# Attention queries split for a two-pass product: the second copy of their high parts, by ScalarE or by a DMA between partitions

## The chip, the cores and the metric

The kernel runs on one core of a Trainium2 chip. The time is that of the device in microseconds for one execution of the whole program; the median of several runs counts. A core has a matrix engine (TensorE, called PE, with its weight loads listed as PEld), a vector engine (VectorE, DVE), an activation engine (ScalarE, ACT), a general engine (GpSimd, POOL) and a queue engine (SyncE, SP) that here issues the DMAs. Each engine works through its own list of instructions in order, and waits on semaphores for the others.

## What is computed

The reference is one step of a streaming encoder layer, in float32: a prompt of 1024 positions, and eight sample sequences of 16 new positions with 1024 cached keys each. Three residual parts follow one another. The edit lies in the first, in the differential attention of the prompt: four heads, each with two maps of 64 columns for queries and keys, whose softmaxes are subtracted.

```python
def diff_attend(q, k, v, bias, mask, lam):
    s = jnp.einsum('bqhmd,bkhmd->bhmqk', q, k).astype(jnp.float32) * (HEAD_DIM ** -0.5)
    s = jnp.where(mask, s + bias[None, :, None], NEG_INF)
    p = jax.nn.softmax(s, axis=-1)
    w = p[:, :, 0] - lam * p[:, :, 1]
    return jnp.einsum('bhqk,bkhe->bqhe', w.astype(v.dtype), v)
...
    h = rmsnorm(x, g_mix)
    z = h @ w_in
    zq, zk, zv, zu = jnp.split(z, [QK_COLS, 2 * QK_COLS, 2 * QK_COLS + ATTN_WIDTH], axis=-1)
    q = rmsnorm(zq.reshape(B, T, N_HEADS, 2, HEAD_DIM), g_q)
    k = rmsnorm(zk.reshape(B, T, N_HEADS, 2, HEAD_DIM), g_k)
...
    o = (rmsnorm(o, g_sub) * (1.0 - lam_init)).reshape(B, T, ATTN_WIDTH)
...
    x = x + jnp.concatenate([o, cv], axis=-1) @ w_out
    x = x + cross_attend(rmsnorm(x, g_cross), mk, mv, w_mq, g_mq, w_mo)
    hf = rmsnorm(x, g_ffn)
    x = x + jnp.square(jax.nn.relu(hf @ w_ff1)) @ w_ff2
```

A mask lets a query see the chunks of 64 up to its own. The samples go through the same attention with their cached keys and values in front.

## The kernel before

**Stages.** Up to about 284 us the input projection and the convolution run. Then comes the attention stage, to about 600 us. Four streams are woven together in it, written as generators: the prompt's attention (`prompt_stream`), the samples' attention (`sample_stream`, eight samples, each reading 2 MB of keys and 2 MB of values), the norm of the convolution (`conv_norm`), and the keys and values of the memory (`memory_stream`). The output projection follows; its convolution half (`pj` out of `wo` and `MT`) needs nothing of the attention and may run before it ends. After it come the cross attention and the MLP.

**Order.** The program is written by a framework that schedules: it takes the instructions as they are written, with priorities, runs them through a timeline of its own, and fixes the order on each engine by when an instruction would be ready there. An edit that changes one instruction's engine or duration can so change the order of others, on all engines, for as long as the streams are woven. At run time the order on an engine is fixed, and an instruction that waits holds up all behind it.

**The prompt's queries and keys.** A float32 product is made of rounded high parts and the low parts that are left. For a head h and a chunk c of 512 positions, `prep_queries` transposes four tiles of queries into one PSUM bank `ps` (`qst`, L619); its partitions 0 to 63 belong to map 0, 64 to 127 to map 1. For map m, with its half `a` of the partitions and the other half `b`, the tile `qs[:, m, :]` holds the scaled high parts twice, in both halves (L639 and L640), and `ql[a, m, :]` the low parts (L641), the rest of `ql` being zero. The keys in `kS[:, m, :]` hold high parts in `a` and low parts in `b` (L628, L629). One matmul of `qs` with `kS` (L674) gives high times high plus high times low at once, and one of `ql` with `kS` (L675) low times high. Both halves of `qs` must so be there before the first of them.

**Tiles of the prompt.** Each head has eight tiles i of 128 queries. `attend` makes two score tiles `sc` (map 0 and 1), adds the bias and finds the maximum on DVE (L679), and takes the exponential on ScalarE (L681); `values` transposes the weights (`pT`, L699), copies them (`wT`, L701) and multiplies by the values (`po`, L704), and stores the result to `mix` (L716). A preparation is made eight times, for each head and each half of its tiles, ahead of tiles 0 and 4.

**Memory.** `wT` lies in a pool (`wk2`) that is opened in the attention stage and takes over the memory of the convolution's accumulators `acc`. The last accumulator is worked on by DVE into the attention stage (L307), and stored to `dacc` (L331) once it is done.

**Samples.** For sample b, `sample_keys` transposes the cached keys (`kT`, L768, one PSUM bank), ScalarE copies them (`ku`, L770), and PE multiplies (`ss`, L777); `sample_weights` and `sample_values` make the weights (`wt`) and the values (`spo`, out of the loads `vu`). The results are stored to `ds`.

The functions that the edit touches, and those that call them:

Of the kernel before, what the change touches and what calls it, by code (L numbers as in the profile page):

```python
# [12 lines left out]
AF = mybir.ActivationFunctionType  # L13
# [46 lines left out]
def f32(ap):  # L60
    return ap.bitcast(F32)
# [3 lines left out]
def kernel(  # L65
# [8 lines left out]
    act, dve, pool, pe, sp = nc.scalar, nc.vector, nc.gpsimd, nc.tensor, nc.sync  # L74
# [357 lines left out]
    gqk = cst.tile([P, 1], F32, name="gqk")  # L432
# [182 lines left out]
    def flipped(r, name):  # L615

        ps = bk("tr", name)
        for j in range(4):
            pe.transpose(ps[:, j * P:(j + 1) * P], r[:, j, :], ident)  # L619
        return ps  # L620
# [11 lines left out]
    def prep_queries(h, c):  # L632

        ps = flipped(halves[0, h, c], f"qst{h}_{c}")
        qs = wk.tile([P, 2, 512], R32, name=f"qs{h}_{c}", tag="qs", bufs=AB["qs"])
        ql = qlow[c]
        for m in range(2):
            a, b = HALF[m], HALF[1 - m]
            act.activation(qs[a, m, :], ps[a], AF.Copy, scale=gqk[a])  # L639
            act.activation(qs[b, m, :], ps[a], AF.Copy, scale=gqk[a])  # L640
            dve.scalar_tensor_tensor(out=ql[a, m, :], in0=ps[a], scalar=gqk[a], in1=f32(qs[a, m, :]),  # L641
                                     op0=ALU.mult, op1=ALU.subtract)
        qss[h, c] = (qs, ql)
        yield
# [6 lines left out]
    def prep(h, c):  # L651

        for wi in (1, 0):
            if (wi, h, c) not in halves:
                load_half(wi, h, c)
        prep_values(h, c)
        yield from prep_keys(h, c)
        yield from prep_queries(h, c)
# [787 lines left out]
    def w1_ops(pr):  # L1446

        raw = []
        for kh in range(2):
            r = next(w1raw).rearrange("p (k c) -> p k c", k=4)  # L1450
            sp.dma_start(r, w_ff1[0, kh * 512:(kh + 1) * 512, pr * 256:(pr + 1) * 256].rearrange("(k p) c -> p k c", p=P))
            raw.append(r)
        a11, a21, a12, a22 = (raw[kh][:, :, f * P:(f + 1) * P] for kh in range(2) for f in range(2))
        s3 = kc(rpool.tile([P, 512], F32, name=f"s3_{pr}", tag="r"))
        ops = {}

        def op(nm, src):
            ops[nm] = wpool.tile([P, 2, 512], R32, name=f"{nm}_{pr}", tag="w")
            split_op(ops[nm].rearrange("p h (k c) -> p h k c", k=4), src)

        if NS <= pr < 16 - NL:
            op("a11", a11)
            op("a12", a12)
        dve.tensor_sub(s3, a11, a21)
        dve.tensor_add(a21, a21, a22)
        dve.tensor_sub(a11, a21, a11)
        op("s2", a11)
        op("s3", s3)
        op("s1", a21)
        op("a22", a22)  # L1470
        dve.tensor_sub(a12, a12, a11)
        op("s4", a12)
        return ops
# [43 lines left out]
    for pr in range(16):  # L1517
# [6 lines left out]
        a = nxt or w1_ops(pr)  # L1524
# [42 lines left out]
    def bank2(name):  # L1567
        return pps.tile([P, 512], F32, name=name, tag="ps")
# [40 lines left out]
    for nm, an, bn, change in STEPS:  # L1609
        ps = [bank2(f"{nm}_{i}") for i in range(4)]  # L1610
# [94 lines left out]
```

## Time and profile before

| | us |
|---|---|
| median of 3 runs | 1568.92 |
| lowest and highest run | 1566.68, 1574.23 |
| profiled execution, its time | 1571.44 |
| profiled execution, span from the first to the last instruction | 1569.7 |

Busy in the span: PE 1496.6 us, DVE 1084.4 us, ScalarE 731.9 us, GpSimd 243.6 us. An engine that is busy only now and then can still be what another waits for. A row of a timeline gives the start and the duration in us, the engine, the line, the operation and the names as out<-in; in square brackets stands how long the engine was idle before it, and what ended the idle time. Rows with SPq are DMAs being issued, and the duration is that of the issue alone.

### The profile page before, as it was taken

How to read it: one execution, taken by the hardware profiler on the slowest of the kernel's cores; microseconds unless marked ns; L12 is line 12 of the kernel's file. 1: busy time of each engine (PE TensorE's matmuls, PEld its weight loads, DVE VectorE, ACT ScalarE, POOL GpSimd, SP SyncE). 2: the span in 40 equal slices, each digit the busy share in tenths (PEclk: the TensorE clock that was granted, in tenths of full speed). 3: DMA queues.
4: the chain of work that ended last, by engine and by line, in shares of the span. 5: the costliest groups of instructions: out<-in, count | busy, mean ns of one | idle time of the engine just before them, and what ended most of it. 6: DMA issues, size and time to landing. Idle time of an engine off the chain costs nothing. (4 is left out here: it accounts for less than half of the span.)

```text
span 1569.7 us, 25622 instructions
## 1 busy us (share of the span) xinstructions
PE 1496.6 (95%) x9326; PEld 1297.6 (83%) x9326; DVE 1084.4 (69%) x2008; ACT 731.9 (47%) x1530; POOL 243.6 (16%) x374
## 2 busy tenths in 40 slices
PE   7999999789898899999999899999999999999999
PEld 7989898557686787887779899999999788878887
DVE  5899899967666564535758786666566556996565
ACT  6312021478677742635656354444353444544342
POOL 3152530041544431131011000000000000000000
PEclk9999999899999999999999999999999999999999
DMA  6423242578774733112432554543574567743443
GB/s 206 139 82 108 87 141 110 170 253 258 231 230 150 254 108 106 46 47 73 155 110 90 166 188 154 160 149 126 167 225 143 173 206 225 237 128 111 122 137 94
DMA packets 187121, 237.88 MB, mean 152 GB/s; under 512 B 23851, under 2 KB 101717, under 8 KB 186996
## 3 DMA queue, kind: packets, MB, share of 16 engines
q1 hardware_dynamic: 186996, 236.25, 47.4%
q8 instruction: 73, 1.20, 0.3%
q14 instruction: 52, 0.43, 0.1%
HBM read 172.59 MB, written 63.60 MB: 150 GB/s over the span
## 5 line engine op out<-in xcount | busy, mean ns | idle before, releaser
L124 PE MATMUL p<-Bp,Ap 128*128 128x512 f32 x448 | 174.9, 390 | 1.1 <-DVE Bp L1573 1.1
L125 PE MATMUL p<-Bp,Ap 128*128 128x512 f32 x448 | 174.2, 389 | 0.0
L123 PE MATMUL p<-Bp,Ap 128*128 128x512 f32 x448 | 157.8, 390 | 1.9 <-ACT Bp L1572 1.9
L307 DVE SCALAR_TENSOR_TENSOR acc<-cp,wc,acc 128x1024 f32<-128x1024 f32 (+2 forms) x150 | 159.1, 1068 | 0.7
L1572 ACT CAST Ap<-w_xb 128x512 fp32r<-128x512 f32 x112 | 69.5, 621 | 160.4 <-PE p L125 133.6
L1573 DVE TENSOR_TENSOR Ap<-w_xb,Ap 128x512 fp32r<-128x512 f32 x112 | 77.8, 694 | 90.2 <-ACT Ap L1572 90.1
L123 PE MATMUL p<-b_t,s 128*128 128x288 f32 x384 | 114.9, 299 | 4.0 <-DVE o L1419 4.0
L125 PE MATMUL p<-b_t,s 128*128 128x288 f32 x384 | 114.6, 299 | 0.5 <-DVE s L1326 0.5
L124 PE MATMUL p<-b_t,s 128*128 128x288 f32 x384 | 114.7, 299 | 0.0
L124 PEld LDWEIGHTS p<-Bp,Ap 128*128 128x128 f32 x448 | 84.1, 188 | 20.5 <-DVE Bp L1573 3.0
L123 PEld LDWEIGHTS p<-Bp,Ap 128*128 128x128 f32 x448 | 83.9, 188 | 19.9 <-ACT Bp L1572 2.7
L125 PEld LDWEIGHTS p<-Bp,Ap 128*128 128x128 f32 x448 | 84.1, 188 | 17.5
L123 PE MATMUL z<-wqkv,h 128*128 128x512 f32 x216 | 86.4, 400 | 0.0
L124 PE MATMUL z<-wqkv,h 128*128 128x512 f32 x216 | 85.5, 396 | 0.0
L125 PE MATMUL z<-wqkv,h 128*128 128x512 f32 x216 | 85.4, 396 | 0.0
L123 PEld LDWEIGHTS p<-b_t,s 128*128 128x128 f32 x384 | 73.2, 191 | 4.7 <-ACT s L1325 4.7
L1409 ACT ACTIVATE o<-o 128x576 f32<-128x576 f32 x64 | 43.9, 686 | 69.0 <-DVE o L1419 28.1
L123 PE MATMUL p<-b_b,a 128*128 128x288 f32 x256 | 75.8, 296 | 0.0
L124 PE MATMUL p<-b_b,a 128*128 128x288 f32 x256 | 75.7, 296 | 0.0
L125 PE MATMUL p<-b_b,a 128*128 128x288 f32 x256 | 75.7, 296 | 0.0
L125 PEld LDWEIGHTS p<-b_t,s 128*128 128x128 f32 x384 | 73.2, 191 | 0.8 <-DVE s L1326 0.8
L124 PEld LDWEIGHTS p<-b_t,s 128*128 128x128 f32 x384 | 73.3, 191 | 0.0
(511 smaller groups left out, 4239.8 us busy)
## 6 DMA issues: line engine op xcount, KB each, us to landing
kr<-in_cache_k_dram SPq DMA_DIRECT2D x32, 512.0 KB
vu<-in_cache_v_dram SPq DMA_DIRECT2D x32, 512.0 KB
w1t<-in_w_ff_dram SPq DMA_DIRECT2D x32, 512.0 KB
w_xb<-ds SPq DMA_DIRECT2D x64, 256.0 KB
da<-o SPq DMA_DIRECT2D x48, 256.0 KB
w_xb<-da SPq DMA_DIRECT2D x48, 256.0 KB
ds<-o SPq DMA_DIRECT2D x32, 256.0 KB
dxr<-XP SPq DMA_DIRECT2D x18, 256.0 KB
```

Source lines behind the costliest of these rows:

```text
L123: pe.matmul(out, lh, rh, start=first, stop=False)
L124: pe.matmul(out, lh, rl, start=False, stop=False)
L125: pe.matmul(out, ll, rh, start=False, stop=last)
L307: dve.scalar_tensor_tensor(out=out, in0=cp[:, lo + j:hi + j], scalar=wj, in1=out, op0=ALU.mult, op1=ALU.add)
L1409: act.activation(c, c, AF.Relu)
L1572: act.copy(u[:, 0], src)
L1573: dve.tensor_sub(u[:, 1], src, f32(u[:, 0]))
```

## The change

The second ScalarE operation on the same PSUM bank goes. In its place SyncE issues a DMA that copies the half `a` of the tile `qs` into its half `b`, from SBUF to SBUF across 64 partitions, 2 KB for each.

```diff
         for m in range(2):
             a, b = HALF[m], HALF[1 - m]
             act.activation(qs[a, m, :], ps[a], AF.Copy, scale=gqk[a])
-            act.activation(qs[b, m, :], ps[a], AF.Copy, scale=gqk[a])
+            sp.dma_start(f32(qs[b, m, :]), f32(qs[a, m, :]))
             dve.scalar_tensor_tensor(out=ql[a, m, :], in0=ps[a], scalar=gqk[a], in1=f32(qs[a, m, :]),
                                      op0=ALU.mult, op1=ALU.subtract)
```

There are 16 such operations, two for each preparation. The order of all engines changes through the attention stage. Three places follow. The numbers in the names are indices of tiles and a running number; `x4` stands for four alike.

The first is on PE, at the preparation ahead of tile 4 of head 2 (`sc_4_0_0_5163`). Before:

```order
L619 MATMUL qst_1_5075<-ident,r_2_1_5013 128x128 x4
L768 MATMUL kT_0_1_1_6068<-ident,kr_1_6049 128x128 x4
L810 MATMUL wt_8_5958<-ident,sp_5525 128x128
L582 MATMUL cvt_5174<-ident,al_5175 128x128 x4
L674 MATMUL sc_4_0_0_5163<-kS_0_4506,qs_1_5080 128x512
```

And with the change:

```order
L619 MATMUL qst_1_5075<-ident,r_2_1_5013 128x128 x4
L810 MATMUL wt_0_6299<-ident,sp_5970 128x128 x4
L582 MATMUL cvt_5174<-ident,al_5175 128x128 x4
L704 MATMUL po_2_4993<-vr_0_4499,wT_2_0_4998 128x128 x3
L810 MATMUL wt_4_6329<-ident,sp_5970 128x128 x4
L674 MATMUL sc_4_0_0_5163<-kS_0_4506,qs_1_5080 128x512
```

Nine matmuls stood between the transposes of the queries and the first score, and now there are 15, of other tiles.

The second is on PE too, about where the values of sample 0 end; `po_0_2829` is the first product of the prompt's weights with its values, `kT_0_1_0_3646` to `kT_1_0_1_3744` are keys of sample 2, `wt` and `spo_3608` belong to sample 1. A piece of the difference:

```order
+L768 MATMUL kT_0_1_0_3646<-ident,kr_1_3643 128x128 x4
+L810 MATMUL wt_0_3444<-ident,sp_3058 128x128 x4
+L768 MATMUL kT_0_1_1_3668<-ident,kr_1_3643 128x128 x4
+L810 MATMUL wt_4_3462<-ident,sp_3058 128x128 x4
+L777 MATMUL ss_0_3553<-ku_0_1_3645,zq 32x256 x4
+L810 MATMUL wt_8_3521<-ident,sp_3058 128x128
+L768 MATMUL kT_1_0_0_3722<-ident,kr_2_3719 128x128 x4
+L825 MATMUL spo_3608<-vu_0_3609,wt_3443 32x128 x8
+L825 MATMUL spo_3608<-vu_2_3689,wt_3443 32x128 x8
+L768 MATMUL kT_1_0_1_3744<-ident,kr_2_3719 128x128 x4
 L704 MATMUL po_0_2829<-vr_0_2752,wT_0_0_2832 128x128
 L699 MATMUL pT_2_0_2943<-ident,p_2_0_2873 128x128 x3
```

The sample rows that came after this place stand ahead of it now.

The third is on SP at the same time in the program: `dacc<-acc_2376` is the store of the last accumulator, `ds<-raw_3335` that of sample 0's result. Before:

```order
L821 DMA vu_6_3321<-in_cache_v_dram 128x2x512
L331 DMA dacc<-acc_2376 128x1024
L821 DMA vu_0_3609<-in_cache_v_dram 128x2x512
L821 DMA vu_2_3689<-in_cache_v_dram 128x2x512
L526 DMA kr_1_3643<-in_cache_k_dram 128x2x512
```

And with the change:

```order
L821 DMA vu_4_3767<-in_cache_v_dram 128x2x512
L831 DMA ds<-raw_3335 8x16x128
L526 DMA kr_2_3719<-in_cache_k_dram 128x2x512
L331 DMA dacc<-acc_2376 128x1024
L101 DMA wmk_2r<-in_w_mk_dram 128x2x256
```

The store has moved behind seven other DMAs, the store of sample 0's result among them.

## Rows read from the trace of the kernel before

**Rows 1.** The page, 40 equal slices of the span, busy tenths.
```profile
PE   7999999789898899999999899999999999999999
DMA  6423242578774733112432554543574567743443
```

**Rows 2.** Stretches of the attention stage: each engine's busy us, granted clock, DMA share, GB/s.
```profile
284.00:330.00 46.00, 31.54 (x265) 20.59 (x265) 38.50 (x68) 25.68 (x59) 11.25 (x15) 0.85 0.62 197
300.00:320.00 20.00, 12.85 (x87) 7.34 (x87) 19.02 (x38) 12.56 (x30) 4.07 (x8) 0.91 0.41 130
330.00:545.00 215.00, 191.48 (x1851) 155.96 (x1850) 143.82 (x383) 162.97 (x389) 89.96 (x145) 0.97 0.72 228
545.00:605.00 60.00, 59.70 (x319) 50.15 (x317) 32.86 (x71) 21.84 (x52) 14.95 (x24) 1.00 0.35 110
```

**Rows 3.** Waits of PE in 284 to 545 us: total, times, longest.
```profile
PE ss L777 <- ACT ku L770: 9.5, 15, 1.6
PE kT L768 <- ACT ku L770: 5.3, 6, 2.1
PE sc L674 <- ACT qs L640: 3.7, 6, 1.3
```

**Rows 4.** The edited line: times in ns (least, median, most), first and last start.
```profile
L640 ACT ACTIVATE qs<-qst,gqk x16: 681/684/685, 286.0 to 544.9; 64x512 fp32r<-64x512 f32 x16
```

**Rows 5.** Timeline of the first preparation.
```profile
284.67 0.38 PE L619 MATMUL qst<-ident,r 128*128 128x128 f32 x2
...
285.35 0.68 ACT L639 ACTIVATE qs<-qst,gqk 64x512 fp32r<-64x512 f32 x1
...
286.04 0.68 ACT L640 ACTIVATE qs<-qst,gqk 64x512 fp32r<-64x512 f32 x1
...
287.40 0.73 DVE L641 SCALAR_TENSOR_TENSOR ql<-qst,gqk,qs 64x512 fp32r<-64x512 f32 x1
...
288.18 1.11 PE L744 MATMUL t<-ident,n 128*128 128x128 f32 x4 [1.08 <-ACT zq L750]
...
288.50 0.68 ACT L639 ACTIVATE qs<-qst,gqk 64x512 fp32r<-64x512 f32 x1
```

**Rows 6.** Stretches around two stores of zt, columns as in rows 2.
```profile
393.00:400.00 7.00, 7.00 (x78) 6.72 (x71) 2.06 (x6) 3.91 (x11) 3.23 (x5) 1.00 0.61 191
505.00:510.00 5.00, 4.81 (x37) 4.14 (x36) 4.29 (x10) 4.63 (x11) 2.89 (x5) 1.00 0.16 52
```

**Rows 7.** Timeline: stores out of SBUF, and what next writes there.
```profile
394.51 1.90 SPq L607 DMA_DIRECT2D dcv<-zt  x1
...
398.79 0.67 ACT L604 ACTIVATE zt<-cvT,hln 128x384 f32<-128x384 f32 x1 [1.69 <-DMA dcv<-zt]
...
507.05 0.34 SPq L607 DMA_DIRECT2D dcv<-zt  x1
...
508.93 0.70 ACT L604 ACTIVATE zt<-cvT,hln 128x384 f32<-128x384 f32 x1
...
602.21 0.32 SPq L716 DMA_DIRECT2D mix<-o  x1
...
605.76 2.00 ACT L133 ACTIVATE HC<-omT,gsub 128x384 fp32r<-128x384 f32 x4 [3.58 <-DMA mix<-o]
...
606.40 0.50 PE L123 MATMUL pj<-wo,HC 128*128 128x512 f32 x1 [1.70 <-ACT HC L133]
```

**Rows 8.** Timeline: the last accumulator's store, and what waits for it.
```profile
323.46 0.41 SPq L331 DMA_DIRECT2D dacc<-acc  x1
...
328.67 0.29 DVE L701 COPY wT<-pT 128x128 f32<-128x128 f32 x1 [4.58 <-DMA dacc<-acc]
...
329.61 0.67 SPq L831 DMA_DIRECT2D ds<-raw  x1
329.67 0.60 PE L619 MATMUL kst<-ident,r 128*128 128x128 f32 x4
...
331.25 0.59 SPq L526 DMA_DIRECT2D kr<-in_cache_k_dram  x1
```

## The prediction

> **What bounds the kernel now.** I read the page first: PE's digits, nines elsewhere, fall from the eighth to the fourteenth of the 40 slices (275 to 549 us), while those of the DMA rise [rows 1]. That is the attention stage. The stretches put numbers to it: from 284 to 330 us PE is busy 31.5 of 46 us, from 330 to 545 us 191.5 of 215 (11% idle, DMA share 0.72), and from 545 to 605 us 59.7 of 60, because matmuls of the output projection fill it [rows 2]. So up to about 545 us the stage is worth what PE's gaps are worth. Who ends them is in the waits of PE: the copies of transposed keys of the sample stream (ku, 9.5 and 5.3 us) come first, and the wait of the scores for the second copy of qs, the edited line, is 3.7 us in six waits [rows 3].
>
> **What the change removes.** Sixteen ScalarE operations (two maps, eight preparations) of 0.684 us each [rows 4], 10.9 us of ScalarE. ScalarE is busy 25.7 + 163.0 of the 261 us [rows 2] and is not the bound, so only two parts count on the path: the 3.7 us for which PE waits for exactly this copy, and 0.7 us at the start, where one copy stands ahead of zq, for which PE waits at 288.18 [rows 5]. The low part ql can start one copy earlier too; that is counted in these waits already. Removed from the path: 4.4 us.
>
> **What it adds: the landing.** In place of 0.68 us a DMA of 64 x 2 KB must be issued and land before the score matmul, which needs both halves. No DMA between partitions stands in the trace, so I bound it by three stores out of SBUF whose source is waited for. A store of zt is issued at 507.05 and zt is written again at 508.93, without a wait: 1.9 us or less, at a DMA share of 0.16 [rows 6, 7]. Another is issued at 394.51 and the writer, held by it, starts at 398.79: 4.3 us, at a share of 0.61 [rows 6, 7]. The last store to mix, half the size of the new DMA, is issued at 602.21 and releases its waiter at 605.76: 3.6 us [rows 7]. I take 3.2, the mean of the three, and keep 1.9 and 4.3.
> The Trainium skill ("DMA: Bandwidth & Descriptors", Anatomy of one DMA) speaks against the swap too: it gives a DMA a fixed 2.0 us, mostly the write receipt, plus bytes over 436 GB/s, in a fit for GpSimd-issued transfers. By it an estimate for 128 KB is 2.3 us, under two of my rows, and the waits below would be 6 us and the sum +3. The rows with a waiter show more than it, and are used.
>
> How much of the landing PE sees depends on what stands between the last query transpose and the first score matmul. ScalarE needs some 0.3 us to start and 0.68 us for the first copy [rows 5], so map 0 is ready 1.0 + 3.2 = 4.2 us after the transposes. Map 1 follows 1.8 us later, since its copy starts after the low part of map 0 (0.73 us, and 0.37 us more till it starts) and takes 0.68 us: 6.0 us. Against it stand the matmuls that PE has in the new order, at 0.11 us for each of 128 columns (four take 0.60, the first of them 0.27) [rows 8]. Before head 2's tile 4 they are 15, or 1.65 us, as the order of the change shows; before head 3's tile 0 they are 17, or 1.9 us; before head 1's tile 4 they are 23, or 2.5 us. For map 1 the cover is 3.1, 2.9 and 5.4 us, with the score matmuls between. Waits: 2.6 + 0.3, 2.3 + 0.8 and 1.7 us, together 7.7. The first preparation has 12 transposes, four of which wait for zq for 3 us anyway [rows 5], so only its map 1 waits, some 1.1 us. The other four preparations have 5 us and more ahead of them, the last one 42 matmuls of 512 columns of the output projection, and wait for nothing. Sum 8.8 us. With a landing of 1.9 us it would be about 4, with 4.3 about 14. PE would have been idle 11% of such time anyway, so 0.89 x 8.8 = 7.8 us remain.
>
> **What it moves.** The scheduler answers the later scores with sample work put first. Where sample 0 ends, PE now does most of sample 2's keys and sample 1's weights ahead of the first values of the prompt (po of tile 0). On SP the store of the last conv accumulator goes behind the store of sample 0's result and a load of kr. That store is no detail: wT, the first tile of a pool that takes over its memory, waits for it, DVE for 4.58 us [rows 8]. It is issued at 323.46 now; the store of ds goes at 329.61 and the load of kr at 331.25 for 0.59 us [rows 8], so it goes at about 331.9, 8.4 us later, and lands 5.2 us after that, as now. Everything of the prompt stream behind wT (values, preparation of chunk 1, tile 4) goes 8.4 us later, and PE has only sample work meanwhile. In 300 to 320 us, where it is much like that, PE is busy 12.85 of 20 us, 36% idle against 11% later [rows 2]: 8.4 x 0.25 = 2.1 us lost. The bounds are 0 (the lead of the samples is used later) and 8.4 (the prompt stream never catches up). By head 3 the two orders are level again, and the last preparation is covered.
>
> The sixteen extra issues cost SP 0.4 us each; SP waits most of the time, and their 2 MB are some 3% of what the stage moves (228 GB/s [rows 2] over 261 us, 60 MB), so nothing is put down for them. Each of these issues waits on SP for ScalarE's first copy, with loads of kr and vu and stores of mix behind it; they are ordered by when they are ready, and a wait of a few tenths there is left at nothing too. On PE transposes of keys, weights and values of the sample stream are queued behind a waiting score, which is why I count its wait in full.
>
> **Sum.** -4.4 + 7.8 + 2.1 = +5.5 us on a profiled execution of 1571.4 us (span 1569.7), so 1577 of that. The median of the runs, 1568.9, is 2.5 us below it: **1575 us**, no change that can be told, on the slow side. A measurement of this kernel can tell about 0.5%, 7.8 us.
>
> **The rivals.**
> *The prompt stream stays late (slower).* PE already waits for the end of that stream: at 606.40 it has sat idle 1.70 us because ScalarE's HC waited for the last store to mix [rows 7]. If the 8.4 us are not made up in the 270 us that follow, they stand whole at that place: -4.4 + 7.8 + 8.4 = +11.8, or 1581 us. It decides from the point where more than 4.4 of the 8.4 us are left. For it: the stream is a chain from tile to tile. Against it: PE has gaps in which it can catch up, and the orders are level by head 3. 24%.
> *Loaded landings (slower).* From 330 to 545 us the DMA share is 0.72 [rows 2], above that of the 4.3 us store. With it at each copy: 0.89 x 14 - 4.4 + 2.1 = +10, or 1579 us. Against it: the two other rows. 11%.
> *ScalarE was the bound after all (faster).* PE's longest waits are for ku, copies that stand behind qs on ScalarE's queue. Were each of the 16 operations on the path, 10.9 us would go; with landings near 1 us, shorter than any row, waits of about 2 us come back: -9, or 1560 us. For it: 14.8 us of ku waits [rows 3]. Against it: ScalarE is busy 163 of the 215 us [rows 2] and has gaps of its own. 13%.
> *Nothing reaches the end.* The waits are swallowed in the gaps, the lead is paid back: 0, or 1569 us. 14%.
> My forecast, a small loss, has 38%, and its own range is 1570 to 1578.
>
> **How the numbers follow.** Slower by over 0.5% begins at 1576.8: the two slow rivals and a tail of the forecast, 0.24 + 0.11 + 0.02 = 0.37. Faster takes most of the fast rival, 0.12. Within 0.5% is the rest, 0.51. The range goes from 1563, which leaves out most of the fast rival, to 1586, beyond both slow ones, with about 0.1 left out at either end.
>
> **What would show it.** In the profile after, 16 rows of ScalarE are gone (10.9 us) and 16 DMAs of qs stand on SP. PE's waits for ACT qs are replaced by waits for a DMA of qs, of some 8 us, most of it before tiles 0 and 4 of heads 2 and 3 and tile 4 of head 1. The store of the accumulator is issued near 332 us and wT starts near 337. The samples run ahead of where they are now, and the prompt's tile 4 of head 0 falls 8 us behind its place. I am wrong if the landings are much shorter than 1.9 us, if wT isn't late, or if the granted clock, 0.85 in 284 to 330 us and 0.97 after [rows 2], moves with the new gaps by more than the gaps themselves.

## The result, and the profile after

The kernel with the DMA takes 1590.86 us (median of four runs, 1588.12 to 1593.02), the kernel before 1571.3 in the same measurement: ratio 1.0124, 95% interval 1.0098 to 1.0150. It is slower by 1.2%, some 20 us, and lies above the forecast range, whose top was 1586. The profiled execution of after took 1593.02 us, its span is 1591.2; of the four it is the longest, and the one with the lowest granted clock over its span, 0.974 (the others 0.976, 0.982 and 0.984). Some executions on one chip, of either kernel, were 25 to 35 us longer, and so were the profiled ones of two experiments (first and second, first to fourth): the ratios leave them out, and these two profiles aren't read.

The page, 40 slices, with what answers to [rows 1]; PE's low digits last no longer than before, so the page shows no new hole that would be the loss:

```profile
PE   6999999788898799999999999999999999999999
DMA  6323232587756551311432554444464566744343
```

The stretches of [rows 2], after:

```profile
284.00:330.00 46.00, 35.92 (x269) 22.87 (x268) 38.91 (x67) 24.76 (x56) 11.01 (x14) 0.70 0.60 196
300.00:320.00 20.00, 15.15 (x90) 9.40 (x89) 17.70 (x37) 12.53 (x30) 5.13 (x8) 0.76 0.36 126
330.00:545.00 215.00, 181.50 (x1778) 148.67 (x1770) 127.46 (x344) 142.22 (x336) 79.08 (x129) 0.94 0.67 213
545.00:605.00 60.00, 56.80 (x268) 45.57 (x267) 40.09 (x93) 29.63 (x78) 23.34 (x32) 0.91 0.57 188
```

The seventh figure from the left after the stretch, the granted clock, is to be read first: 0.85, 0.97 and 1.00 in [rows 2] have become 0.70, 0.94 and 0.91. The same stretch doesn't hold the same work in the two kernels, so the stage is also cut by its work: from the first transposes of keys to the first matmul of the projection's second half (606.40 in [rows 7]). Before:

```profile
283.95:606.40 322.45, 282.77 (x2431) 226.76 (x2431) 215.24 (x522) 211.13 (x499) 116.19 (x183) 0.96 0.63 201
```

and after:

```profile
284.75:627.40 342.65, 296.59 (x2430) 236.20 (x2430) 214.60 (x521) 202.16 (x483) 116.23 (x183) 0.91 0.61 195
```

It is the same work on PE, 2431 and 2430 matmuls. The stage is 20.2 us longer, which is the loss (0.8 us stand ahead of it, 0.5 behind). In this execution PE is busy 13.8 us longer with the same matmuls, at a lower granted clock, and idle 6.4 us longer (46.1 against 39.7). ScalarE is relieved by 9 us, and the stage isn't shorter for it.

PE's waits in 284 to 545 us, answering to [rows 3]:

```profile
PE sc L674 <- DMA qs<-qs: 9.8, 6, 1.8
PE ss L777 <- ACT ku L770: 8.4, 10, 1.7
PE kT L768 <- ACT ku L770: 4.5, 10, 1.1
```

The waits for qs were 3.7 us and are 9.8; those for ku fell by 1.9 us in all. A timeline of after shows landings from the issue to the score that waits, at the preparations ahead of tile 4 of head 0, tile 0 of head 1 and tile 0 of head 3:

```profile
344.23 0.50 SPq L640 DMA_DIRECT2D qs<-qs  x1
...
351.67 0.50 PE L674 MATMUL sc<-kS,qs 128*128 128x512 f32 x1 [1.78 <-DMA qs<-qs]
...
390.67 1.40 SPq L640 DMA_DIRECT2D qs<-qs  x2
...
400.07 0.33 PE L674 MATMUL sc<-kS,qs 128*128 128x128 f32 x1 [1.29 <-DMA qs<-qs]
...
538.28 0.54 SPq L640 DMA_DIRECT2D qs<-qs  x1
...
542.99 0.33 PE L674 MATMUL sc<-kS,qs 128*128 128x128 f32 x1 [1.71 <-DMA qs<-qs]
```

That is 7.4, 9.4 and 4.7 us from issue to release. The stretches between these, columns as in [rows 2], and those of the two waits ahead of tile 4 of head 1 (4.8 and 5.6 us) show how busy the DMA engines were; the sixth landing, ahead of tile 4 of head 2, took 5.6 us at a share of 0.95:

```profile
344.23:351.67 7.44, 3.89 (x58) 2.71 (x56) 2.04 (x6) 5.38 (x12) 1.58 (x4) 1.00 1.09 328
390.67:400.07 9.40, 7.25 (x81) 4.83 (x81) 4.21 (x12) 6.11 (x14) 1.62 (x4) 1.00 1.05 336
429.13:433.89 4.76, 2.64 (x26) 1.84 (x24) 1.58 (x4) 4.71 (x9) 2.84 (x3) 1.00 0.90 276
433.19:438.76 5.57, 3.11 (x24) 2.06 (x25) 2.17 (x7) 4.40 (x11) 3.39 (x4) 1.00 0.71 220
538.28:542.99 4.71, 2.25 (x17) 1.77 (x18) 1.70 (x3) 3.13 (x7) 1.44 (x3) 1.00 0.97 306
```

The accumulator's store and what waits for it, answering to [rows 8]:

```profile
329.77 0.67 SPq L831 DMA_DIRECT2D ds<-raw  x1
...
331.00 0.45 SPq L331 DMA_DIRECT2D dacc<-acc  x1
...
337.69 0.29 DVE L701 COPY wT<-pT 128x128 f32<-128x128 f32 x1
```

The prompt is late from here on, and gets later: the store of head 1's last tile (the sixteenth to mix) was issued at 463.94, 180.0 us behind the first transposes, and is now issued at 487.52, 202.8 us behind them. Before:

```profile
463.94 0.33 SPq L716 DMA_DIRECT2D mix<-o  x1
```

After:

```profile
487.52 0.33 SPq L716 DMA_DIRECT2D mix<-o  x1
```

### The profile page after: what moved, and what is told of

Read it like the earlier page. It is cut to its first block, busy times and chain, and to the rows that moved or that the text cites. A ratio compares the mean times of both kernels' runs of the same rounds, so it can differ in the third digit from the quotient of the medians.

```text
span 1591.2 us, 25643 instructions
## 1 busy us (share of the span) xinstructions
PE 1511.1 (95%) x9326; PEld 1307.9 (82%) x9326; DVE 1083.8 (68%) x2008; ACT 723.0 (45%) x1514; POOL 245.4 (15%) x374
```

## The experiments

Three theories. *Gaps and clock*: the scores wait for the landing, PE stands, and its granted clock falls. *Order*: the scheduler's new order costs it, whoever copies. *Traffic*: 16 issues and 2 MB more delay other transfers.

**Traffic alone.** ScalarE's copy is kept, and the same half is stored to DRAM, where nobody reads it.

```diff
             act.activation(qs[b, m, :], ps[a], AF.Copy, scale=gqk[a])
+            sp.dma_start(dqd[m], f32(qs[a, m, :]))
```

> ScalarE makes both copies as before; beside it the same half of qs is stored to a DRAM tensor that nobody reads, 16 times 64 x 2 KB from SP. Gaps and clock (the cost is that scores wait for the landing, and that the granted clock falls in the gaps): no score waits for a DMA, so within 0.4% of before, 1565 to 1577 us. Traffic (16 issues on SP and 2 MB delay the other transfers): most of the 19 us is there, 1583 us or more. Order (any edit that changes the scheduler's order costs as much): a loss too, 1578 us or more, with the order of PE changed through the stage.

Measured: 1569.02 us, ratio 1.0001 (0.9987 to 1.0015). No cost of the traffic shows; that theory falls. The profile of this run shows one thing more, in its stage and in the first stretch of it, up to the first store to mix:

```profile
284.25:605.94 321.69, 286.75 (x2430) 229.15 (x2430) 214.80 (x522) 211.14 (x499) 115.75 (x183) 0.94 0.65 208
284.25:336.65 52.40, 39.36 (x285) 25.91 (x285) 40.33 (x72) 27.43 (x62) 12.94 (x17) 0.71 0.59 194
```

The granted clock is lower than before, and PE is busy 4.0 us longer, but idle 4.7 us less, and the stage is no longer. Longer busy time at a lower clock is thus not by itself a loss.

**Queries one tile earlier**, with the DMA and with ScalarE's copy. The rest of a preparation stays where it was (the load of the queries, not shown, goes with them).

```diff
+            if i % 4 == 2 and n + 2 < len(tiles):
+                its.append(prep_queries(tiles[n + 2][0], tiles[n + 2][1] // 4))
             if i % 4 == PA and n + 4 - PA < len(tiles):
...
         yield from prep_keys(h, c)
-        yield from prep_queries(h, c)
```

> The DMA as in the change, but the queries of a preparation are transposed and split one tile earlier than its keys, so that the landing has several us of other work ahead of it (the first preparation can't be moved). Gaps and clock: the waits of PE for the DMA of qs fall from 9.8 us to under 2 us, the granted clock returns to that of before, 0.96 or so over the stage, and the time to 1568 to 1578 us. Order: another order, and the loss stays, 1583 us or more. Traffic: the loss stays, 1585 us or more, though the waits are gone.

> The ScalarE copy of before with the queries one tile earlier, the partner of the run with the DMA. Gaps and clock: the 3.7 us of waits for the copy go, and the time is that of before or 3 us less, 1564 to 1572 us; the DMA with the same early queries is then within 0.5% of this. Order: an arbitrary other order, off from before by up to 20 us either way. If this one is slower than before by as much as the change is, the place of the queries or the order counts, and not who copies.

Measured: with the DMA 1570.42 us (1.0010, 0.9994 to 1.0025), with ScalarE 1562.59 (0.9946, 0.9928 to 0.9965). With cover the DMA's loss against before is gone; against its own partner, ScalarE's copies with the same early queries, 7.8 us are left. The landings aren't all covered. Waits with the DMA:

```profile
PE sc L674 <- DMA qs<-qs: 4.8, 5, 1.5
```

and with ScalarE's copies, where the last to come is now a low part of the keys:

```profile
PE sc L674 <- DVE kS L629: 3.5, 5, 1.3
...
PE sc L674 <- ACT qs L642: 1.3, 1, 1.3
```

**Fillers**, in the change and in the kernel before: eight matmuls of 512 columns ahead of the first score of each preparation, 64 in all; the score overwrites what they leave.

```diff
+                if m == 0 and c == 0 and i % 4 == 0:
+                    for _ in range(8):
+                        pe.matmul(b, ql[:, m, :], kSs[h][c][:, m, :], start=True, stop=True)
                 pe.matmul(b[:, :n], qs[:, m, :], kS, start=True, stop=False)
```

> The DMA as in the change, with eight matmuls of 512 columns out of ql and kS into the score bank ahead of the first score of each preparation (their result is overwritten by the score): PE has 1.8 us of extra work, 64 matmuls and 14 us in all at full clock, in the place of the wait for the landing. Gaps and clock: the waits for the DMA of qs fall to 2 us or less, and if the lower granted clock came from these gaps it rises from 0.90 to 0.94 or more over the stage, and the time falls below that of the change, 1578 to 1588 us, in spite of the work. If the gaps cost time but not clock: as the change, 1588 to 1594 us. Order: 1590 us and more, the 14 us of work on top.

> The control of the run with fillers: ScalarE's copies as before, with the same 64 matmuls of 512 columns ahead of the first scores. Gaps and clock: there is little to fill here (3.7 us of waits for the copy, 27 us at the lower clock in the stage), so the 14 us of work cost 8 to 14 us, 1578 to 1585 us, while in the change they cost less than nothing. If fillers are a gain or free here too, they do something other than close the gaps that the landings leave.

Measured: in the change 1583.02 us (1.0090, 1.0056 to 1.0125), by the ratios 0.34% less than without the extra work, though the two intervals overlap: two of the four executions took 1578 to 1579 us and two 1587 to 1588. In the kernel before 1571.60 (1.0017, 1.0001 to 1.0033), 2.5 us more than without. The stage of the first, cut as above, in one of its two longer executions (1588.18 us):

```profile
282.42:625.40 342.98, 300.65 (x2494) 238.14 (x2494) 219.24 (x520) 203.26 (x483) 114.91 (x183) 0.96 0.62 195
```

Eight fillers take 2.1 us, as a row of its timeline shows:

```profile
460.10 2.12 PE L676 MATMUL sc<-kS,ql 128*128 128x512 f32 x8
```

That makes 17 us for 64 (the 1.8 and 14 us of the expectation were too little). Against the profile of the change PE's busy time rose by 4 us alone, because the granted clock is 0.96, that of before, and no longer 0.91; its idle time is 42.3 us in place of 46.1. The waits for qs fell to 5.5 us, not to 2. The stage is as long as in the change (343.0 against 342.7), at the clock of before. So 17 us of work were put into it at no cost, but that it became shorter isn't clear of the noise. In the kernel before the same work is nearly free too, which I had not expected. By the words of the expectation the fillers then do something other than close the gaps that the landings leave, and the pair is no proof that these gaps, or the clock behind them, are the loss.

**One part of the eight preparations at a time**, by a condition on head h and half c; the others by ScalarE as before. PE's order is that of the change, word for word, up to the first preparation that differs from it.

```diff
+            if (h, c) == (0, 0):
+                sp.dma_start(f32(qs[b, m, :]), f32(qs[a, m, :]))
+            else:
+                act.activation(qs[b, m, :], ps[a], AF.Copy, scale=gqk[a])
```

First alone: 

> Only the first preparation (head 0, first half) makes its second copy by a DMA, the other seven by ScalarE. Gaps and clock: what the change lost at the start of the stage (zq 1.9 us late, the lower granted clock for 17.1 us in place of 10.2 behind it, and 0.9 us more in 284 to 288 us) is 4 to 5 us, so 1570 to 1577 us, and the later score waits are those of ScalarE's copies, some 2.5 us. Order: the order of the scheduler already differs from here on, and a loss of 10 us and more is possible without any later landing.

All but the first: 

> The first preparation by ScalarE, the other seven by the DMA. Gaps and clock: the five later preparations whose scores wait for the landing keep 8 to 10 us of waits, and the granted clock falls behind several of them; 1580 to 1590 us, that is most of the loss of the change less the 4 to 5 us of its start. Order: anything from 1570 to 1595 us, whatever the waits are.

Second to fourth: 

> Only three preparations by the DMA: those ahead of tile 4 of head 0, tile 0 of head 1 and tile 4 of head 1, where the change waited 6.5 of its 9.8 us; all others by ScalarE. Gaps and clock: most of the loss of the run with seven such preparations (0.55%) is here, 1574 to 1584 us. If the waits do not set the time, it lies within 0.3% of before.

First, and heads 2 and 3: 

> The counterpart: the first preparation and the four of heads 2 and 3 by the DMA, the three others by ScalarE. In the change two waits, 3.2 us, lie here, and the first preparation by itself costs nothing. Gaps and clock: 1570 to 1578 us. Order: this and its counterpart do not add up to the change, and either may be slow.

First to fourth: 

> The four preparations of heads 0 and 1 by the DMA, those of heads 2 and 3 by ScalarE; PE's order is that of the change up to tile 0 of head 2. If the missing 11 us arise where the samples, put first behind the first preparation, meet the landings of heads 0 and 1: 1583 to 1590 us, with the prompt's last tile of head 1 stored 200 us or more behind the start of the stage, as in the change (202.8; before 180.0). If the parts add up: 1572 to 1576 us.

First and second: 

> The two preparations of head 0 by the DMA, all others by ScalarE; PE's order is that of the change up to tile 0 of head 1. If the landing ahead of tile 4 of head 0, with the DMA engines full (7.4 us there in the change), starts the loss: 1576 to 1584 us, and the last tile of head 0 is stored some 125 us behind the start of the stage (before 106.6). If the loss needs the other two of head 1: 1569 to 1574 us.

All but the second: 

> All but the second preparation (ahead of tile 4 of head 0) by the DMA. If this landing starts the loss, it falls by half and more: 1574 to 1581 us. If each preparation adds its wait alone: 1586 to 1590 us, 2 to 4 us less than the change.

All but the third: 

> All but the third preparation (ahead of tile 0 of head 1, the longest landing of the change, 9.4 us) by the DMA; the order is that of the change up to there. If this landing makes the loss: 1574 to 1581 us. If each adds its wait alone: 1586 to 1590 us.

Measured against the kernel before (the preparations numbered in the order of the program):

| preparations by the DMA | ratio | 95% interval |
|---|---|---|
| 1 | 0.9999 | 0.9982 to 1.0016 |
| 1, 2 | 1.0044 | 1.0023 to 1.0064 |
| 1 to 4 | 1.0079 | 1.0046 to 1.0111 |
| 1 to 8 (the change) | 1.0124 | 1.0098 to 1.0150 |
| 2 to 4 | 1.0025 | 1.0010 to 1.0040 |
| 1, 5 to 8 | 1.0026 | 1.0011 to 1.0041 |
| 2 to 8 | 1.0055 | 1.0039 to 1.0071 |
| 1, 3 to 8 | 1.0061 | 1.0037 to 1.0084 |
| 1, 2, 4 to 8 | 1.0085 | 1.0050 to 1.0119 |

Of the expectations, given in us, the ratios make 1576.9 (first and second), 1582.4 (first to fourth), 1579.6 (all but the second) and 1583.3 us (all but the third) on the 1570 of before. The first preparation costs nothing: my expectation of 4 to 5 us was wrong. All but the first took 1578.92 us, a little less than the 1580 to 1590 expected. Second to fourth (1574.24) and first with heads 2 and 3 (1574.50) lie within what was expected, the former at its lower end. The parts don't add up: the first to fourth come close to the 1583 to 1590 expected if the samples, put first, meet the landings of heads 0 and 1, and lie far above 1572 to 1576. The loss grows along the chain: 0.44% with the second, 0.35% more with the third and fourth, 0.45% more with the last four. It isn't one place. Taken out of the change, the second gives back 0.63% and the third 0.39%; by their intervals the two can't be told apart. Without the first ahead of them the second to fourth cost 0.25%, against 0.80% behind it.

The run without the second preparation has a profile at the clock of before:

```profile
284.66:613.62 328.96, 283.28 (x2430) 226.14 (x2430) 216.30 (x522) 203.20 (x485) 112.74 (x183) 0.96 0.64 202
```

PE is as busy as before (283.3 against 282.8 us), and the stage is 6.5 us longer, 6.0 of it idle time: a loss at an equal clock.

In the run of the second to fourth, the landing ahead of tile 4 of head 0 is as long as in the change, 7.5 us from issue to score:

```profile
337.98 3.28 SPq L641 DMA_DIRECT2D qs<-qs  x2
...
345.45 0.50 PE L677 MATMUL sc<-kS,qs 128*128 128x512 f32 x1 [0.45 <-DMA qs<-qs]
```

but PE waits 0.45 us for it and not 1.78, since more work stands in front (5.8 us of it between issue and score, in place of 3.9). The wait depends on what the order leaves as cover, and not on the landing alone.

**GpSimd's copy**, from the one half of qs into the other, no DMA.

```diff
-            sp.dma_start(f32(qs[b, m, :]), f32(qs[a, m, :]))
+            pool.tensor_copy(qs[b, m, :], f32(qs[a, m, :]))
```

> The second copy as a GpSimd copy from SBUF to SBUF, of the same half of qs into the other: ScalarE is relieved as by the DMA, without a landing behind the loads. Gaps and clock: if GpSimd needs 1 to 2 us for 64 x 512, a wait of 1 to 2 us stays at a few preparations, 3 to 6 us in all, and the time is 1566 to 1576 us. Order: the scheduler's order is new here too, and the loss is that of the change, 1583 us or more.

Measured: 1576.37 us (1.0045, 1.0029 to 1.0062). A copy takes 0.6 us, and no score waits for one. PE waits elsewhere:

```profile
PE kT L768 <- ACT ku L770: 11.8, 9, 3.9
PE ss L777 <- ACT ku L770: 9.4, 10, 3.0
```

That is 21 us for ku, against 14.8 in [rows 3]. ScalarE is relieved as in the change, there is no landing, and it is still 0.45% slower. Its order differs from that of before and from that of the change, so it shows that a new order can cost this much, but not how much the order of the change costs.

**The DMA from ScalarE's queue.** PE's order is that of the change up to tile 4 of head 1.

```diff
-            sp.dma_start(f32(qs[b, m, :]), f32(qs[a, m, :]))
+            act.dma_start(f32(qs[b, m, :]), f32(qs[a, m, :]))
```

> The DMA of the change, issued from ScalarE's queue in place of SP's. The order on PE is that of the change, word for word, up to tile 4 of head 1; only the queue differs that carries the 128 KB. Landings (the wait comes from standing behind the loads of kr and vu that SP issued before): the DMA overtakes them, PE waits for it less than 4 us in all in place of 9.8, and the time is 1573 to 1583 us. If the share of the DMA engines sets the landing, whatever the queue, the waits stay at 8 us or more and the time at 1586 to 1594 us. Order: as the change, 1586 us and more, with short waits.

Measured: 1593.90 us (1.0149, 1.0130 to 1.0168). The waits for qs are 10.3 us. The landing of the second map ahead of head 1 takes 8.2 us, much as from SP, where the first map's took 9.4:

```profile
391.33 0.47 ACTq L640 DMA_DIRECT2D qs<-qs  x1
...
399.56 0.33 PE L674 MATMUL sc<-kS,qs 128*128 128x128 f32 x1 [1.02 <-DMA qs<-qs]
```

So the landing isn't much shorter from another queue, and standing behind the loads in SP's own queue isn't the reason for it; the share of the DMA engines is 1.01 in this stretch too. The Trainium skill ("Perfetto Trace Analysis", DMA Optimizations) says that balancing DMAs over several issuing engines may help where making descriptors is the bottleneck. In this run nothing was gained by it. This run's profile also shows how the loss divides:

```profile
287.21:630.30 343.09, 291.93 (x2430) 232.50 (x2430) 216.03 (x522) 203.88 (x483) 117.36 (x183) 0.93 0.61 195
```

The stage is as long as in the change (343.1 against 342.7), but PE is busy 9.2 us longer than before and idle 11.5 us longer.

**A faster kernel?** ScalarE's copies, queries early, and the keys and values of each head's second half early too.

```diff
             if i % 4 == 2 and n + 2 < len(tiles):
                 its.append(prep_queries(tiles[n + 2][0], tiles[n + 2][1] // 4))
+            if i == 2 or i == 7 and n + 1 < len(tiles):
+                its.append(prep(h if i == 2 else h + 1, int(i == 2)))
```

> A try for a faster kernel: ScalarE's copies of before with the queries one tile earlier, and the keys and values of the second half of each head one tile earlier too, since in the run with early queries alone PE waits 3.5 us for the keys' low parts. If these waits are on the path, 1557 to 1563 us; if they are swallowed, as the run with early queries alone, 1560 to 1565 us.

Measured: 1561.26 us (0.9949, 0.9932 to 0.9966), the same as with early queries alone. Both are half a per cent faster than the kernel before.

## Why the prediction was wrong

**What was removed.** Right: the 16 operations are gone, and ScalarE does less. The 0.7 us that were to be gained at the first preparation are there too:

```profile
288.15 0.66 PE L744 MATMUL t<-ident,n 128*128 128x128 f32 x4 [1.87 <-ACT zq L750]
```

The wait for zq is longer, 1.9 us in place of 1.1, because the score that stood ahead of it now comes later. But these transposes start 3.4 us behind the first transposes of the stage (284.75), and no longer 4.2. The 3.7 us of waits for the copy went as well; the waits for the landing stand in their place.

**The landing** (3.2 us, the mean of three stores). Mis-sized: 4.7 to 9.4 us in the six waits. The bounds of 1.9 and 4.3 us came from stores in stretches with a share of 0.16 and 0.61 [rows 6]; four of the landings took 4.7 to 5.6 us at shares of 0.71 to 0.97, and two took 7.4 and 9.4 us at 1.09 and 1.05. The estimate of 2.3 us by the Trainium skill ("DMA: Bandwidth & Descriptors", Anatomy of one DMA) is farther off still. That PE's waits, 9.8 us, came near the 8.8 forecast is luck: the landing and the cover were both longer, and the places were in part others. Tile 4 of heads 1 and 2 and tile 0 of head 3 were right. Map 1 of the first preparation didn't wait. The two waits ahead of tile 4 of head 0 and tile 0 of head 1, 3.1 us together, stand where "the other four preparations" were to wait for nothing.

**What was moved** (2.1 us). This is the step that failed. Its beginning was right to the microsecond: the store issued at 331.00 (forecast 331.9) and wT at 337.69 (337). But the prompt was to catch up, with the lead of the samples used later, the orders level by head 3, and 2.1 of 8.4 us lost. The stage, cut at the first store to mix and at the last stores of heads 0, 1 and 2, shows that it didn't. Before:

```profile
283.95:331.94 47.99, 33.52 (x283) 21.97 (x284) 40.02 (x72) 27.13 (x62) 12.12 (x17) 0.86 0.63 205
331.94:390.52 58.58, 53.68 (x572) 41.73 (x572) 44.23 (x127) 48.48 (x120) 13.79 (x30) 1.00 0.83 264
390.52:463.94 73.42, 64.96 (x641) 53.99 (x641) 48.54 (x125) 53.47 (x125) 36.11 (x56) 0.98 0.72 229
463.94:534.06 70.12, 61.52 (x576) 51.27 (x574) 40.57 (x108) 50.76 (x119) 33.76 (x50) 0.93 0.57 180
534.06:606.40 72.34, 69.09 (x369) 57.81 (x367) 41.89 (x91) 31.29 (x77) 20.42 (x31) 1.00 0.45 142
```

After:

```profile
284.75:343.05 58.30, 46.69 (x384) 30.32 (x385) 42.34 (x78) 33.08 (x73) 16.24 (x20) 0.74 0.70 231
343.05:409.98 66.93, 57.95 (x624) 45.58 (x624) 44.14 (x131) 46.12 (x116) 11.13 (x28) 0.97 0.80 253
409.98:487.52 77.54, 68.66 (x660) 58.20 (x660) 47.81 (x129) 53.92 (x126) 37.36 (x58) 0.93 0.67 213
487.52:553.08 65.56, 49.60 (x394) 40.77 (x392) 37.77 (x97) 38.04 (x93) 31.29 (x47) 0.89 0.50 156
553.08:627.40 74.32, 73.70 (x375) 61.33 (x375) 42.55 (x89) 31.00 (x78) 20.20 (x32) 0.96 0.40 130
```

The prompt is 10.3 us late at its first store, 18.7 at the end of head 0 and 22.8 at the end of head 1; the stage ends 20.2 us late. The prompt's own matmuls are the same in both kernels, 42 and 153 in the first two stretches. What has grown there is the work of the samples, from 241 and 379 matmuls to 342 and 431 (counted by their lines, L744 to L825). That work is missing in the stretch of head 2, where 125 of the samples' matmuls are left of 278. There PE is idle 16.0 us of 65.6 (3.2 of them for qs), before 8.6 of 70.1. I read this so: the samples' work drawn forward holds the prompt up, and later PE has too little beside the prompt, so the lead isn't paid back. The lower clock of the first stretch, 0.74 for 0.86, has a share in the first 10 us.

The late start alone isn't the loss. With the first preparation alone by the DMA, whose order is that of the change up to there, 342 of the samples' matmuls stand ahead of the first store too. The stage is no longer than before, and head 1's last store stands 185.2 us behind the first transposes (470.12), between before and the change:

```profile
470.12 0.33 SPq L719 DMA_DIRECT2D mix<-o  x1
```

In that run 209 of the samples' matmuls are left for head 2. All but the second leaves 161 and loses 0.61%, all but the third 157 and 0.85%, the change 125 and 1.24%. But with early queries and the DMA 157 are left too, and no loss against before: the order goes with the loss, and isn't shown to be its only cause.

The rival that the prompt stays late came true in that the delay stands to the end. Its place was wrong: PE was to wait for the last store at 606.40 [rows 7], and in the profile after, the first matmul of the projection's second half (627.43) waits for nothing. PE is busy 73.7 of the last 74.3 us; the time was lost before.

**The clock.** The sum counted gaps, +5.5 us, and has no term for a changed clock, which the prediction named as able to make it wrong. In the profiled execution the idle time grew by 6.4 us, close to the sum, and the busy time by 13.8. But this is the execution with the lowest clock, and the others show that the clock is the smaller part. At 0.982 and 0.984 over the span the change took 1588.12 and 1589.87 us. The kernel before, in the runs made beside the experiments, took 1574.81 and 1575.24 us at 0.982, and 1568.77 to 1572.07 at 0.984. So 13 to 21 us of the loss are left at an equal clock. A straight line through the 87 executions of before that the ratios of the experiments use (0.981 to 0.991) gives 0.77 us for each 0.001 of clock. By that the 0.009 by which the change's mean is lower make some 7 of the 20 us, an estimate. That the idle time came near the sum is then luck of this execution.

A fall behind two waits for qs, at 433.89 (1.71 us) and 438.76 (1.75 us), shows a clock that falls behind landings (before, in and behind the fall):

```profile
430.00:439.00 9.00, 5.12 (x39) 3.66 (x38) 3.09 (x10) 7.54 (x17) 6.17 (x7) 1.00 0.77 236
439.07:442.47 3.40, 3.40 (x17) 2.89 (x19) 1.53 (x5) 1.54 (x5) 0.47 (x2) 0.50 0.26 14
442.50:452.00 9.50, 8.87 (x109) 6.94 (x103) 8.61 (x26) 5.79 (x13) 1.86 (x4) 1.00 0.91 311
```

PE was busy 5.1 of 9 us, then runs at 0.50, 1.2 GHz in place of 2.4. The Trainium skill ("TensorE: Matmul & The Clock Gate", The HAM clock gate) describes a gate that halves the clock after too little activity; these rows agree. About half of the low clock isn't the landing's doing, though: the 58.3 us up to the first store to mix, at 0.74, lie before any wait for qs. The run with the unread store has 0.71 there, without a loss, and the first preparation alone, with the same order on PE, 0.91:

```profile
284.92:338.91 53.99, 39.01 (x382) 25.03 (x382) 41.98 (x78) 32.68 (x73) 15.85 (x20) 0.91 0.77 252
```

**What stays open.** How the loss divides between idle time and clock isn't fixed: 6.4 and 13.8 us in this execution, 11.5 and 9.2 in that of the run from ScalarE's queue. How it divides between the order and the waits for the landing isn't either. Shown: the traffic by itself has no effect that can be told; with queries early the DMA takes the time of before, and 7.8 us more than ScalarE's copies with queries early; the parts cost more together than one by one; a new order without any landing (GpSimd) costs 0.45%; most of the loss stands at an equal clock. A run with the order of the change and ScalarE's copies, which would give the order's share alone, wasn't made: the scheduler makes another order when the copying engine changes.

## What to carry to other kernels

Take an operation off an engine only where that engine ends a wait. A DMA in its place adds a landing, and the landing is to be read from stretches with the DMA share of the place where it will stand. Where a scheduler draws other work forward to cover it, look at what that work holds up, and at whether enough is left for later; a delay isn't made up by itself. One profiled execution can put on the clock what the others, at a higher clock, lose too: compare executions at an equal clock before the clock is called the cause. If something must land before a score, start it a tile earlier: that was worth half a per cent here with ScalarE's copies, and with the DMA it brought back the time of before.

## What the runs showed of the hardware

The 64 x 2 KB from SBUF to SBUF were released 4.7 to 5.6 us after their issue in four of the six waits, at DMA shares of 0.71 to 0.97, and 7.4 and 9.4 us after it at 1.09 and 1.05. From ScalarE's queue one took 8.2 us at 1.01, and another 5.3 us at the same share, so the share alone doesn't set it. 64 matmuls of 512 columns, 17 us of work, put ahead of the scores made the kernel before 2.5 us longer, and the stage of the change no longer. GpSimd's copy of 64 x 512 from one half of the partitions to the other took 0.6 us.
